# Loading weight blocks half a block before they are split, in a hybrid attention and retention layer

## The chip, the cores and the metric

The kernel runs on one core of a Trainium2 chip. The metric is the device time of one execution in microseconds (us), the median of several timed runs. The engines are TensorE (PE in the profile, with PEld for its weight loads), VectorE (DVE), ScalarE (ACT), GpSimd (POOL) and SyncE (SP), which here does nothing but issue transfers.

## The reference, cut to what matters

One decoder layer on a sequence of 1024 tokens with 1024 features, all float32:

```python
u = rmsnorm(x, norm_pre_w)
proj = u @ w_in                              # 1024 x 4096, eight parts of 512 columns
dq, dk, dv, dg, rq, rk, rv, rg = split(proj)
y_a = diff_attention(rotary(dq), rotary(dk), dv)   # 4 heads, two softmaxes each: p1 - lam * p2
y_a = rmsnorm(y_a, diff_subln_w) * (1 - lambda_init) * silu(dg)
y_b = retention(rotary(rq), rotary(rk), rv)        # 4 heads, chunks of 128 tokens, a state per chunk
y_b = rmsnorm(y_b) * silu(rg)
out = x + rmsnorm(concat(y_a, y_b) @ w_out, norm_post_w)
```

## The kernel before

Every float32 operand of a large product is split in two parts, hi (a cast to the type fp32r) and lo (the rest), and the product is three matmuls: hi by hi, lo by hi, hi by lo. The input tokens are split once (uh, ul, in two halves of 512 tokens).

The weights come in 16 blocks of 256 columns, in the order ORDER; a block is either values and gates of a head (part 0, `rows_steps`, matmuls of 256 columns) or queries and keys (part 1, `cols_steps`, matmuls of 512 columns). A block is four chunks of 256 KB. `load_chunk` issues the transfer of a chunk into one of four `raw` buffers, has ACT cast it to `whi`, and has DVE or POOL in turn subtract to get `wlo`. `whi` and `wlo` have eight buffers each, that is two blocks: a cast for block b+1 writes buffers that the matmuls of block b-1 read. `main_steps` calls `load_block(b + 1)` at the start of block b and then runs `block_steps(b)`, four groups g of matmuls, each into one PSUM bank.

The order of the instructions on PE and on SP's queue is the order of emission, which a planner in the kernel decides. It keeps an estimated time `clock[0]`, an estimate of SP's queue `queue[0]` (0.6 us for each transfer), and for each of the eight PSUM banks the estimated time at which it is free (`bank`, `give`). `run` takes `main_steps` as filler and puts steps of four side streams in as soon as they are due: `score_stream` (q by k matmuls, masked max, exponentials, the combined p), `value_stream` (`diff_turn` transposes p on PE at L524, `diff_values` multiplies by the values), `ret_stream` (retention: `ret_scores`, `ret_states`, `ret_out` at L617) and `last_stream` (`prep_tile` transposes finished rows, L672, for the output product of `out_steps`). Due times are `st["due", i]`, `due` and `st["y", t]`. The order on ACT, DVE and POOL is made by the compiler's own simulated schedule. All queues are in order: an instruction that waits holds those behind it.

Blocks 0 and 1 are emitted before `run`, with the planner's clock at 0 throughout. After the rotation of a query and key block, 24 small transfers (`moves` in `diff_qk`) per half of the tokens put hi and lo parts in place for the scores; they are held back by 4.0 us of estimated time (`late(4.0, moves)`). The output weights are loaded by `fetch_wout` and split by `split_wout` (`load_wout` is both); those of the first half of the output columns, `nh` 0, take over the buffers of uh0 and ul0, which the second group of block 15 is the last to read.

Of the kernel before, what the change touches and what calls it, by code (L numbers as in the profile page):

```python
# [10 lines left out]
F32 = mybir.dt.float32  # L11
# [9 lines left out]
P = 128  # L21
# [64 lines left out]
def body(ctx, tc, x, xt_in, pos, wpk, wout, vecs, npre, npost, subln, cst, out):  # L86
# [12 lines left out]
    wraw = pool("wraw", 4)  # L99
# [74 lines left out]
        eng = nc.vector if lo_turn[0] % 4 in (1, 2) else nc.gpsimd  # L174
        eng.tensor_tensor(dst, full, hi.bitcast(F32), op=ALU.subtract)  # L175

    def load_chunk(b, c, pieces=1):

        raw = wraw.tile([P, 2, 256], F32, tag="raw", name="raw")
        hi = whi.tile([P, 2, 256], F32R, tag="whi", name="whi")  # L180
        lo = wlo.tile([P, 2, 256], F32R, tag="wlo", name="wlo")
        for k in range(pieces):
            ks = slice(2 // pieces * k, 2 // pieces * (k + 1))
            dma(raw[:, ks, :], wpk[b, :, 2 * c + ks.start:2 * c + ks.stop, :])
            nc.scalar.copy(hi[:, ks, :], raw[:, ks, :])  # L185
            split_lo(lo[:, ks, :], raw[:, ks, :], hi[:, ks, :])
        return hi, lo

    def load_block(b):
        return [load_chunk(b, c) for c in range(4)]  # L190

    def weight(parts, kt):
        return tuple(part[:, kt % 2, :] for part in parts[kt // 2])
# [262 lines left out]
    def diff_scores(st, i, u):  # L456
# [52 lines left out]
        e1 = sm_.tile([P, 1], F32, tag="e1", name="e1")  # L509
        nc.vector.scalar_tensor_tensor(e1, s1, EPS, s1, op0=ALU.mult, op1=ALU.mult)  # L510
        st["p", i] = (p1, e1)
        st["due", i] = softmax[0] + 1.0

    def head_ms(o_ps, ms, scale):
        sq = sqp.tile([P, P], F32, tag="sq", name="sq")
# [197 lines left out]


    heads = [{"h": hh} for hh in HEADS]
    blocks = {}
    done = set()
    def block_steps(b):
        n, part = ORDER[b]
        st = heads[n]  # L720
        w = blocks[b]
        for g in range(4):

            if part == 0 and n > 2 and g == 0:
                yield lambda: ("A", n - 3) in done or ("R", n - 3) in done
            if part == 1 and n > 1 and g == 1:
                yield lambda: ("S", n - 2) in done or ("R", n - 2) in done
            if part == 0:
                ps = yield from rows_steps(w, g)
                values_gates(st, g, ps)  # L730
                st["values", g] = clock[0] + 1.44 + 1.6
                yield 1.44
            else:
                ps = yield from cols_steps(w, g % 2, g // 2)
                (diff_qk if st["h"] < H else ret_qk)(st, g, ps)
                yield 1.36
            if b == NB - 1:
                if g == 0:
                    load_wout(1, range(0, 4))
                elif g == 1:  # L740
                    load_wout(0, range(8))
                    fetch_wout(1, range(4, 8))
        blocks.pop(b)

    def main_steps():
        for b in range(2, NB):
            n, part = ORDER[b]
            if b + 1 < NB:
                blocks[b + 1] = load_block(b + 1)
            yield from block_steps(b)  # L750
        split_wout(1, range(4, 8))
        for t in range(NT):
            yield lambda: fp.get(("ready", t), 1e9) <= clock[0]
            yield from out_steps(t)
            done.add(("out", t))
# [35 lines left out]
    def ret_stream():  # L791
        for n, st in enumerate(heads):
            if st["h"] < H:
                continue
            for t2 in range(4):
                yield lambda: max(st.get(("ready", t2 // 2), 1e9), st.get(("values", t2), 1e9)) <= clock[0] and \
                    banks(2) and (n < 7 or "y" in fp and (t2 < 2 or ("prep", 2 * t2 - 3) in done))
                if n == 7:
                    load_y(2 * t2)
                    load_y(2 * t2 + 1)  # L800
                ret_scores(st, t2)
                due = clock[0] + 0.66 + 2.0
                yield 0.66
                yield lambda: due <= clock[0]
                ret_states(st, t2)
                due = clock[0] + 0.44 + 3.0
                yield 0.44
                yield lambda: due <= clock[0] and banks(1)
                ret_out(st, t2)
                for t in (2 * t2, 2 * t2 + 1):  # L810
                    st["y", t] = clock[0] + 0.88 + 4.5
                yield 0.88
            done.add(("R", n))

# [16 lines left out]
    def run(main, sides):  # L831

        sides = [[s, None] for s in sides]
        queue[0] = 8.0
        wait = None

        def advance(s):
# [33 lines left out]
    with tc.tile_pool(name="xin", bufs=6) as xin, tc.tile_pool(name="xp", bufs=1) as xp, tc.tile_pool(name="tp", bufs=1) as tp:  # L871
# [19 lines left out]
        for c in range(4):  # L891
            if c == 0:
                load_u(xin, 0, 0, 1)
                w0.append(load_chunk(0, c, 2))
                load_u(xin, 0, 1, 1)
            else:
                w0.append(load_chunk(0, c))
                load_u(xin, 0, 2 * c, 2)
        first = proj_rows(w0, [0, 1], [bank("pj"), bank("pj")])
        for c in range(4):  # L900
            load_u(xin, 1, 2 * c, 2)
        second = proj_rows(w0, [2, 3], [bank("pj"), bank("pj")])
        blocks[1] = load_block(1)
        dma(cs, cst)
        for half in range(2):
            dma(posi[64 * half:64 * half + 64, :], pos[half].partition_broadcast(64))
# [16 lines left out]
        nc.gpsimd.affine_select(out=tri, in_=tri, compare_op=ALU.is_ge, fill=0.0, base=0,  # L923
                                pattern=[[1, P]], channel_multiplier=-1)

        blocks[2] = load_block(2)
        for k, _ in enumerate(block_steps(1)):
            if k == 7:
                ec, es = angles(tp, posi, cs)
            if k == 11:  # L930
                tables(tp, ones, ec, es)
                nc.vector.tensor_scalar(wo["s"], sub, 0.5 * (1.0 - LAM_INIT), None, op0=ALU.mult)
                lambdas(tp, lv)
# [63 lines left out]
```

## Time and profile before

| what | value |
|---|---|
| time, median of 3 runs | 602.39 us (599.98 to 604.27) |
| the profiled execution: its own time, its span | 599.01 us, 597.3 us |
| PE busy | 575.7 us, 96% of the span |
| DVE, ACT, POOL busy | 52%, 41%, 23% |
| HBM, mean over the span | 77 GB/s |
| granted PE clock, mean | 0.994 |
| chain that ended last: PE, SP's queue, transfers | 77%, 7%, 7% |

PE is the engine to look at; the others matter where they make it wait. A row of a timeline shows in brackets how long its engine was idle before that instruction and what ended the wait.

### The profile page before, as it was taken

How to read it: one execution, taken by the hardware profiler on the slowest of the kernel's cores; microseconds unless marked ns; L12 is line 12 of the kernel's file. 1: busy time of each engine (PE TensorE's matmuls, PEld its weight loads, DVE VectorE, ACT ScalarE, POOL GpSimd, SP SyncE). 2: the span in 40 equal slices, each digit the busy share in tenths (PEclk: the TensorE clock that was granted, in tenths of full speed). 3: DMA queues.
4: the chain of work that ended last, by engine and by line, in shares of the span. 5: the costliest groups of instructions: out<-in, count | busy, mean ns of one | idle time of the engine just before them, and what ended most of it. 6: DMA issues, size and time to landing. Idle time of an engine off the chain costs nothing.

```text
span 597.3 us, 10157 instructions
## 1 busy us (share of the span) xinstructions
PE 575.7 (96%) x3664; PEld 521.0 (87%) x3664; DVE 307.9 (52%) x780; ACT 243.4 (41%) x700; POOL 136.1 (23%) x182
## 2 busy tenths in 40 slices
PE   6998997999999999999999999999999989999995
PEld 5998876999889988999899888899988988888884
DVE  3882247675542678522427784437585345443232
ACT  5796124355411664424026643126643454222120
POOL 3170133331321322312213223223220101000000
PEclk9999999999999999999999999999999999999998
DMA  8941645700214532212145332146401476243222
GB/s 274 371 162 36 175 103 151 181 19 19 80 27 105 156 103 58 74 46 81 36 122 128 97 98 54 32 101 156 119 16 39 122 247 215 71 151 121 73 72 105
DMA packets 41490, 65.62 MB, mean 110 GB/s; under 512 B 7136, under 2 KB 14688, under 8 KB 41440
## 3 DMA queue, kind: packets, MB, share of 16 engines
q1 hardware_dynamic: 41296, 64.97, 37.9%
q8 instruction: 29, 0.48, 0.3%
q14 instruction: 21, 0.17, 0.1%
q10 hardware_dynamic: 144, 0.00, 0.0%
HBM read 38.21 MB, written 7.86 MB: 77 GB/s over the span
## 4 chain that ended last, share of the span: by engine, by line
PE 77%; SPq 7%; DMA 7%; DVE 3%; ACT 2%; issue 2%; POOL 1%; DVEq 0%; POOLq 0%; ACTq 0%
PE pj L346 7%; PE pj L348 7%; PE pj L347 7%; SPq L123 7%; PE pj L360 7%; PE pj L362 7%; PE pj L361 7%; PE op L694 5%; PE op L692 5%; PE op L693 5%; PE sc L468 5%; PE o L537 5%; DMA raw<-in_wpk 4%; PE pj L329 3%; PE tp L524 3%; DMA raw<-in_wout 2%
## 5 line engine op out<-in xcount | busy, mean ns | idle before, releaser
L346 PE MATMUL pj<-whi,uh 128*128 128x256 f32 x448 | 129.4, 289 | 0.0
L348 PE MATMUL pj<-whi,ul 128*128 128x256 f32 x448 | 126.7, 283 | 0.0
L347 PE MATMUL pj<-wlo,uh 128*128 128x256 f32 x448 | 126.6, 283 | 0.0
L360 PE MATMUL pj<-uh,whi 128*128 128x512 f32 x256 | 103.0, 402 | 1.7 <-DVE gt L380 1.7
L362 PE MATMUL pj<-uh,wlo 128*128 128x512 f32 x256 | 100.5, 392 | 0.0
L361 PE MATMUL pj<-ul,whi 128*128 128x512 f32 x256 | 100.3, 392 | 0.0
L165 POOL TENSOR_TENSOR tot<-tot,halves 128x1 f32<-128x1 f32 (+1 forms) x56 | 34.2, 611 | 263.2 <-DVE tot L164 263.2
L346 PEld LDWEIGHTS pj<-whi,uh 128*128 128x128 f32 x448 | 85.6, 191 | 0.5 <-issue 0.2
L347 PEld LDWEIGHTS pj<-wlo,uh 128*128 128x128 f32 x448 | 85.7, 191 | 0.4
L348 PEld LDWEIGHTS pj<-whi,ul 128*128 128x128 f32 x448 | 85.6, 191 | 0.0
L175 POOL TENSOR_TENSOR wlo<-raw,whi 128x512 fp32r<-128x512 f32 x32 | 43.3, 1362 | 74.4 <-ACT whi L185 70.7
L185 ACT CAST whi<-raw 128x512 fp32r<-128x512 f32 (+1 forms) x65 | 39.1, 616 | 51.4 <-DMA raw<-in_wpk 44.4
L360 PEld LDWEIGHTS pj<-uh,whi 128*128 128x128 f32 x256 | 48.6, 190 | 11.0 <-DVE gt L380 1.9
L362 PEld LDWEIGHTS pj<-uh,wlo 128*128 128x128 f32 x256 | 48.3, 189 | 10.4
L361 PEld LDWEIGHTS pj<-ul,whi 128*128 128x128 f32 x256 | 48.6, 190 | 9.2
L493 ACT ACTIVATE p<-sc,nm 128x384 f32<-128x384 f32 (+5 forms) x48 | 27.6, 579 | 57.2 <-DVE nm L472 55.5
L692 PE MATMUL op<-woh,yh 128*128 128x512 f32 x128 | 50.8, 396 | 0.0
L694 PE MATMUL op<-woh,yl 128*128 128x512 f32 x128 | 50.0, 390 | 0.0
L693 PE MATMUL op<-wol,yh 128*128 128x512 f32 x128 | 49.9, 389 | 0.0
L468 PE MATMUL sc<-ks,qs 128*128 128x384 f32 (+5 forms) x192 | 43.3, 353 | 0.8 <-DMA qs<-rlo 0.8
L424 POOL TENSOR_TENSOR o<-o,m 128x512 f32<-128x512 f32 x16 | 25.9, 1622 | 77.1 <-DVE o L421 77.0
L698 ACT ACTIVATE osq<-op 128x512 f32<-128x512 f32 x16 | 9.6, 598 | 70.7 <-PE op L694 70.7
(138 smaller groups left out, 977.3 us busy)
## 6 DMA issues: line engine op xcount, KB each, us to landing
raw<-in_wpk SPq DMA_DIRECT2D x63, 256.0 KB, 4.4
xr<-in_x SPq DMA_DIRECT2D x8, 512.0 KB, 7.1
qs<-rhi SPq DMA_DIRECT2D x64, 64.0 KB, 2.0
qs<-rlo SPq DMA_DIRECT2D x64, 64.0 KB, 2.0
raw<-in_wout SPq DMA_DIRECT2D x16, 256.0 KB, 3.6
xt<-in_x SPq DMA_DIRECT2D x8, 512.0 KB, 3.6
out<-ob SPq DMA_DIRECT2D x16, 256.0 KB, 2.4
xk<-in_xt SPq DMA_DIRECT2D x7, 512.0 KB, 7.8
```

Source lines behind the costliest of these rows:

```text
L123: nc.sync.dma_start(dst, src)
L175: eng.tensor_tensor(dst, full, hi.bitcast(F32), op=ALU.subtract)
L346: nc.tensor.matmul(dst, lhsT=a, rhs=wh, start=(kt == 0 and j == 0), stop=False)
L347: nc.tensor.matmul(dst, lhsT=a, rhs=wl, start=False, stop=False)
L348: nc.tensor.matmul(dst, lhsT=b, rhs=wh, start=False, stop=(kt == KT - 1 and j == 1))
L360: nc.tensor.matmul(ps, lhsT=wh, rhs=uh[half][:, kt, :], start=(kt == 0), stop=False)
L361: nc.tensor.matmul(ps, lhsT=wh, rhs=ul[half][:, kt, :], start=False, stop=False)
L362: nc.tensor.matmul(ps, lhsT=wl, rhs=uh[half][:, kt, :], start=False, stop=(kt == KT - 1))
L468: nc.tensor.matmul(sp[:, 0:kn], lhsT=st["q"][:, u, x, i * P:(i + 1) * P], rhs=st["k"][:, u, k0:k0 + kn], start=(x == 0), stop=(x == 1))
L692: nc.tensor.matmul(op, lhsT=yh[:, m, :], rhs=wh, start=(m == 0), stop=False)
L693: nc.tensor.matmul(op, lhsT=yh[:, m, :], rhs=wl, start=False, stop=False)
L694: nc.tensor.matmul(op, lhsT=yl[:, m, :], rhs=wh, start=False, stop=(m == 7))
```

## The change

The transfer and the split of a chunk become two functions, `fetch_chunk` and `split_chunk`. The split of block b+1 stays at the start of block b; the transfers of block b+2 are issued in block b ahead of its third group (g == 2). The raw buffers stay four. For the output weights: chunks 0 to 3 of the second column half (`nh` 1) are fetched in block 14 and split at the start of block 15, and chunks 0 to 3 of the first column half are fetched after the first group of block 15 and split after its second. In block 1 the planner's clock now advances with the steps, and `run` shifts the banks' free times and starts again at 0. Three estimates are longer: p is due 0.5 us later, the retention output of the last head 1.0 us later, finished rows 1.5 us later.

```diff
--- before.py
+++ after.py
@@ -174,20 +174,31 @@
         eng = nc.vector if lo_turn[0] % 4 in (1, 2) else nc.gpsimd
         eng.tensor_tensor(dst, full, hi.bitcast(F32), op=ALU.subtract)
 
-    def load_chunk(b, c, pieces=1):
-
-        raw = wraw.tile([P, 2, 256], F32, tag="raw", name="raw")
+    raws, blocks = {}, {}
+
+    def fetch_chunk(b, c, pieces=1):
+
+        raw = raws[b, c] = wraw.tile([P, 2, 256], F32, tag="raw", name="raw")
+        for k in range(pieces):
+            ks = slice(2 // pieces * k, 2 // pieces * (k + 1))
+            dma(raw[:, ks, :], wpk[b, :, 2 * c + ks.start:2 * c + ks.stop, :])
+
+    def split_chunk(b, c, pieces=1):
+        raw = raws.pop((b, c))
         hi = whi.tile([P, 2, 256], F32R, tag="whi", name="whi")
         lo = wlo.tile([P, 2, 256], F32R, tag="wlo", name="wlo")
         for k in range(pieces):
             ks = slice(2 // pieces * k, 2 // pieces * (k + 1))
-            dma(raw[:, ks, :], wpk[b, :, 2 * c + ks.start:2 * c + ks.stop, :])
             nc.scalar.copy(hi[:, ks, :], raw[:, ks, :])
             split_lo(lo[:, ks, :], raw[:, ks, :], hi[:, ks, :])
         return hi, lo
 
-    def load_block(b):
-        return [load_chunk(b, c) for c in range(4)]
+    def fetch_block(b):
+        for c in range(4):
+            fetch_chunk(b, c)
+
+    def split_block(b):
+        blocks[b] = [split_chunk(b, c) for c in range(4)]
 
     def weight(parts, kt):
         return tuple(part[:, kt % 2, :] for part in parts[kt // 2])
@@ -509,7 +520,7 @@
         e1 = sm_.tile([P, 1], F32, tag="e1", name="e1")
         nc.vector.scalar_tensor_tensor(e1, s1, EPS, s1, op0=ALU.mult, op1=ALU.mult)
         st["p", i] = (p1, e1)
-        st["due", i] = softmax[0] + 1.0
+        st["due", i] = softmax[0] + 1.5
 
     def head_ms(o_ps, ms, scale):
         sq = sqp.tile([P, P], F32, tag="sq", name="sq")
@@ -713,13 +724,17 @@
 
 
     heads = [{"h": hh} for hh in HEADS]
-    blocks = {}
     done = set()
     def block_steps(b):
         n, part = ORDER[b]
         st = heads[n]
         w = blocks[b]
         for g in range(4):
+
+            if g == 2 and b + 2 < NB:
+                fetch_block(b + 2)
+            elif g == 2 and b + 2 == NB:
+                fetch_wout(1, range(0, 4))
 
             if part == 0 and n > 2 and g == 0:
                 yield lambda: ("A", n - 3) in done or ("R", n - 3) in done
@@ -736,9 +751,10 @@
                 yield 1.36
             if b == NB - 1:
                 if g == 0:
-                    load_wout(1, range(0, 4))
+                    fetch_wout(0, range(0, 4))
                 elif g == 1:
-                    load_wout(0, range(8))
+                    split_wout(0, range(0, 4))
+                    load_wout(0, range(4, 8))
                     fetch_wout(1, range(4, 8))
         blocks.pop(b)
 
@@ -746,7 +762,9 @@
         for b in range(2, NB):
             n, part = ORDER[b]
             if b + 1 < NB:
-                blocks[b + 1] = load_block(b + 1)
+                split_block(b + 1)
+            else:
+                split_wout(1, range(0, 4))
             yield from block_steps(b)
         split_wout(1, range(4, 8))
         for t in range(NT):
@@ -803,12 +821,12 @@
                 yield 0.66
                 yield lambda: due <= clock[0]
                 ret_states(st, t2)
-                due = clock[0] + 0.44 + 3.0
+                due = clock[0] + 0.44 + (4.0 if n == 7 else 3.0)
                 yield 0.44
                 yield lambda: due <= clock[0] and banks(1)
                 ret_out(st, t2)
                 for t in (2 * t2, 2 * t2 + 1):
-                    st["y", t] = clock[0] + 0.88 + 4.5
+                    st["y", t] = clock[0] + 0.88 + 6.0
                 yield 0.88
             done.add(("R", n))
 
@@ -831,7 +849,9 @@
     def run(main, sides):
 
         sides = [[s, None] for s in sides]
-        queue[0] = 8.0
+        for k in range(8):
+            free[k] -= clock[0]
+        clock[0], queue[0] = 0.0, 8.0
         wait = None
 
         def advance(s):
@@ -891,16 +911,19 @@
         for c in range(4):
             if c == 0:
                 load_u(xin, 0, 0, 1)
-                w0.append(load_chunk(0, c, 2))
+                fetch_chunk(0, c, 2)
+                w0.append(split_chunk(0, c, 2))
                 load_u(xin, 0, 1, 1)
             else:
-                w0.append(load_chunk(0, c))
+                fetch_chunk(0, c)
+                w0.append(split_chunk(0, c))
                 load_u(xin, 0, 2 * c, 2)
         first = proj_rows(w0, [0, 1], [bank("pj"), bank("pj")])
         for c in range(4):
             load_u(xin, 1, 2 * c, 2)
         second = proj_rows(w0, [2, 3], [bank("pj"), bank("pj")])
-        blocks[1] = load_block(1)
+        fetch_block(1)
+        split_block(1)
         dma(cs, cst)
         for half in range(2):
             dma(posi[64 * half:64 * half + 64, :], pos[half].partition_broadcast(64))
@@ -923,8 +946,10 @@
         nc.gpsimd.affine_select(out=tri, in_=tri, compare_op=ALU.is_ge, fill=0.0, base=0,
                                 pattern=[[1, P]], channel_multiplier=-1)
 
-        blocks[2] = load_block(2)
-        for k, _ in enumerate(block_steps(1)):
+        fetch_block(2)
+        split_block(2)
+        for k, cost in enumerate(block_steps(1)):
+            clock[0] += cost
             if k == 7:
                 ec, es = angles(tp, posi, cs)
             if k == 11:
```

## Rows read from the trace of the kernel before

**Rows 1.** Stretches of 15 us: length, busy (PE, PEld, DVE, ACT, POOL), clock, DMA share, GB/s

```profile
0.00:15.00 15.00, 9.72 (x59) 9.02 (x59) 6.03 (x10) 9.01 (x15) 4.92 (x14) 1.00 0.82 274
...
90.00:105.00 15.00, 11.30 (x48) 9.10 (x47) 10.62 (x32) 6.81 (x19) 5.92 (x4) 0.89 0.56 147
...
585.00:600.00 15.00, 6.05 (x27) 4.69 (x25) 3.00 (x6) 1.38 (x4) 0.55 (x1) 0.79 0.19 69
sum 600.00, PE 575.68 PEld 520.97 DVE 307.87 ACT 243.39 POOL 136.06; mean PE 14.39 PEld 13.02 DVE 7.70 ACT 6.08 POOL 3.40
```

**Rows 2.** Timeline of PE, the matmuls that it waited for after 15 us

```profile
57.67 0.50 PE L360 MATMUL pj<-uh,whi 128*128 128x512 f32 x1 [1.69 <-DVE gt L380]
...
83.11 0.30 PE L468 MATMUL sc<-ks,qs 128*128 128x128 f32 x1 [0.61 <-DMA qs<-rlo]
...
100.87 0.33 PE L524 MATMUL tp<-ident,p 128*128 128x128 f32 x1 [3.70 <-DVE p L508]
...
164.31 1.38 PE L524 MATMUL tp<-ident,p 128*128 128x128 f32 x8 [1.11 <-DVE p L508]
...
412.25 0.30 PE L524 MATMUL tp<-ident,p 128*128 128x128 f32 x1 [0.40 <-DVE e L510]
...
486.79 1.20 PE L672 MATMUL yt<-ident,yt 128*128 128x128 f32 x9 [0.72 <-DVE yt L396]
...
489.36 0.49 PE L617 MATMUL o<-v,sT 128*128 128x128 f32 x2 [1.15 <-DVE sT L594]
```

**Rows 3.** One stretch of 1 us, PE alone: length, busy, clock, DMA share, GB/s

```profile
102.00:103.00 1.00, 1.00 (x4) 0.50 0.64 141
```

**Rows 4.** Timelines of DVE and POOL ahead of the longest wait

```profile
93.47 0.69 DVE L175 TENSOR_TENSOR wlo<-raw,whi 128x512 fp32r<-128x512 f32 x1 [2.11 <-ACT whi L185]
...
95.28 0.29 DVE L472 CUSTOM_DVE_ANT_0 sc<-sc,mask 128x128 f32<-128x128 f32 x1
...
97.31 1.71 POOL L424 TENSOR_TENSOR o<-o,m 128x512 f32<-128x512 f32 x1
...
97.82 1.74 DVE L175 TENSOR_TENSOR wlo<-raw,whi 128x512 fp32r<-128x512 f32 x1
...
100.48 0.73 DVE L508 SCALAR_TENSOR_TENSOR p<-sc,cn,p 128x128 f32<-128x128 f32 x2
```

**Rows 5.** Timeline of SP's queue: issues of transfers

```profile
69.03 2.02 SPq L123 DMA_DIRECT2D raw<-in_wpk  x4
74.00 0.57 SPq L123 DMA_DIRECT2D ks<-rhi  x1
...
89.18 2.02 SPq L123 DMA_DIRECT2D raw<-in_wpk  x4
91.29 0.51 SPq L123 DMA_DIRECT2D ks<-rhi  x1
```

**Rows 6.** Transfers of one kind: count, KB each, median us to landing

```profile
qs<-rlo SPq DMA_DIRECT2D x64, 64.0 KB, 2.0
```

**Rows 7.** Who waited for whom: us in total, times, longest

```profile
POOL wlo L175 <- ACT whi L185: 70.7, 18, 9.5
...
ACT whi L185 <- DMA raw<-in_wpk: 44.4, 21, 15.7
```

**Rows 8.** The chain that ended last, 152 to 165 us: start, us, what

```profile
152.21 5.28 DMA raw<-in_wpk
...
158.27 3.08 POOL wlo L175 x2
...
163.60 0.67 DVE p L508
```

**Rows 9.** Timelines of ACT and DVE in block 15

```profile
484.96 2.71 ACT L651 ACTIVATE woh<-raw,wos 128x512 fp32r<-128x512 f32 x4 [3.90 <-DMA raw<-in_wout]
...
486.39 0.60 DVE L396 SCALAR_TENSOR_TENSOR yt<-o,tot,gt 128x128 f32<-128x128 f32 x2
...
488.89 0.41 DVE L594 TENSOR_TENSOR sT<-rs,tri 128x256 f32<-128x256 f32 x1
```

## The prediction

> **What bounds the kernel now.** I read the stretches first. Over the span of 597.3 us PE is busy 575.68 us [rows 1], so all that a change of order can give back lies in 21.6 us. Of those, 5.28 us are in the first 15 us (15.00 less 9.72, the first loads and splits) and 6.25 us at the end (the last stretch ends with the span after 12.30 us, 6.05 of them busy: the last evacuation and store) [rows 1]. The change touches neither, which leaves 10.1 us. The timeline of PE names them: seven waits of 1.69, 0.61, 3.70, 1.11, 0.40, 0.72 and 1.15 us, together 9.38 us [rows 2]; the rest are crumbs. One of them costs more than its length: in the stretch from 90 to 105 us the mean granted clock is 0.89, and right after the wait of 3.70 us it is 0.50, the lower of the two levels [rows 1, 3]. 0.11 of 15 us is 1.65 us of full-speed work that was lost. So the ceiling is 10.1 + 1.65, some 11.7 us or 2% of the kernel. What a reader is to see: 96% busy doesn't say where a gain can be; the bracketed waits do.
>
> Then I asked who holds PE up. The releaser is mostly DVE with the combined p, never a weight itself: after the start no weight load or split stands as the releaser of a matmul in these rows. Weights cost in another way. ACT stood 44.4 us, 21 times, before a cast whose transfer had not landed, once for 15.7 us, and POOL 70.7 us before the subtractions that follow [rows 7]. The queues are in order, so exponentials, row statistics and rotations stand behind those casts. The chain that ended last shows one such case whole: a weight transfer of 5.28 us, two subtractions of POOL in 3.08 us, then a row statistic, a scaling, and only then the p for which PE waits at 164 us [rows 8, 2].
>
> **The change part by part.** *Banks.* At 57.67 us, the first matmul of block 2, PE waits 1.69 us for the gates of block 1's last group [rows 2]. With the clock at 0 all banks of blocks 0 and 1 carry nearly the same free time, and the lowest number wins, which is the bank just used. With the clock running, block 2 opens with a bank whose reader belongs to block 0 and is long done. I take 1.6 us; ends 0 and 1.69. It is plain filler time, nothing else feeds those matmuls.
>
> *Loads of blocks 3 and up, around 57 to 107 us.* Here SP's queue is the critical chain. Four loads issue at 69.03 in 2.02 us, then nothing until 74.00, since the first `moves` need a cast that stands on ACT behind the casts of the weights just requested; 24 moves then take 89.18 - 74.00 = 15.18 us, 0.63 us each; then four more loads, and the next 24 moves begin at 91.29 [rows 5]. After the change the loads of block 3 are issued in block 1, where SP has little to do before the tables. The place at 69.03 goes to block 4's loads, whose buffers the early splits of block 3 have emptied. ACT is then not blocked, and the moves can start at 69.03 + 2.02 = 71.05, 2.95 us earlier. The four loads between the two sets of moves are gone, so the second set starts at 71.05 + 15.18 = 86.2, 5.1 us earlier than 91.29. A move lands some 2.0 us after its issue [rows 6]; the first score, which now waits 0.61 us, needs the twelfth: 71.05 + 12 x 0.63 + 2.0 = 80.6, while PE, 1.69 us earlier, comes to it at about 83.11 - 0.61 - 1.69 = 80.8. I take 0.3 us gained, ends 0 and 0.61.
>
> The wait at 100.87: DVE's score work starts at 95.28, after a subtraction at 93.47 for which DVE stood 2.11 us; then a second one, 1.74 us long, stands ahead of the statistics, and p is made at 100.48 [rows 4]. Freed of the waiting, and with the rotation buffers released some 3 us earlier, DVE can start the maxima 3 to 5 us earlier and p follows near 96. PE comes to the transpose at 100.87 - 3.70 = 97.2, less 1.7 for the banks and 0.3, plus 0.5 for the later due time: 95.7. So nearly all 3.70 us go, and with them the clock's 1.65. I take 4.9 of 5.35; the low end is 1.5, if only part of the wait goes and the clock falls all the same.
>
> *The same elsewhere.* The wait of 1.11 us at 164.31 goes: the transfer of 5.28 us leaves the chain [rows 8], four times the wait's length. I take 1.1, ends 0 and 1.11. The wait of 0.40 us at 412.25 I give whole, ends 0 and 0.40 [rows 2].
>
> *Block 15.* PE's waits of 0.72 and 1.15 us [rows 2] have one cause: ACT stands 3.90 us before the first output weights at 484.96, DVE stands behind it with their lo parts, and the scaling of the rows at 486.39 and the masked scores at 488.89 come late [rows 9]. The row names a transfer as releaser, but the casts write buffers that the second group of block 15 still reads, so I read PE as the true releaser. The earlier fetch can't help there. What helps are the estimates: the retention output 1.0 us later and finished rows 1.5 us later put block 15's own matmuls in PE's way instead. I take 1.7 of 1.87, the low end is 0. There is filler: the two remaining groups of block 15.
>
> **What it adds.** No arithmetic is added; the number of transfers is the same. (1) A fetch now waits on SP for raw buffers, that is for the splits of the block before; behind it on SP's queue stand row stores and the moves of the first half. In the chain of rows 8 the transfer, the idle time and the subtractions end at 161.35, 9.1 us after the transfer began, and half a block of matmuls plus the side streams is over 10 us; with the transfer gone from it the margin grows. I cost it at 0, ends 0 and 2. The late start of the moves (4.0 us of estimate) covers the four issues, 2.02 us [rows 5]. (2) A cast now waits only for the matmuls of the block before, no longer for data, so four casts and four subtractions come in a bunch at each block's start. A subtraction on DVE takes 0.69 us alone and 1.74 beside POOL [rows 4].
>
> The Trainium skill ("GPSIMD Engine Reference", section 8, Key points) says that POOL shares its SBUF interfaces with VectorE, in contention with VectorE instructions of two SBUF inputs, which a subtraction is. That speaks against bunching, and these two rows agree with it; by the rule the term of the next sentence would stand at its upper end of 3 us, and the sum below at 6.5 us instead of 9.0.
>
> Two DVE subtractions a block cost 2 x 1.05 = 2.1 us more if both collide. DVE is busy 307.87 of 597.3 us [rows 1], so I let PE see 0.5 us in all, ends 0 and 3. (3) With PE some 8 us earlier, the scores of the second half of the tokens come up against SP's queue: its last move issues at 86.2 + 15.2 = 101.4. No row prices that; between 0 and the landing of one move, 2.0 [rows 6], I take 0.5.
>
> *Sum.* 1.6 + 0.3 + 4.9 + 1.1 + 0.4 + 1.7 = 10.0 gained, 1.0 given back: 9.0. The profiled execution took 599.0 us, 590.0 after. The median of the runs is 602.39, 0.56% above the profiled one; 590.0 x 1.0056 = 593.3, say 593. A change of 1% is 6.0 us, about what three runs between 599.98 and 604.27 can tell from none.
>
> **The rivals.** *Half of it.* SP's queue stays the bound up to 107 us: PE no longer waits at 100.87 for p, but the order on DVE is simulated anew and may still put a collided subtraction ahead. 2 us of that wait stay and the clock still falls (1.7 gained instead of 4.9), the second half's scores wait the full 2.0, the rest holds: 10.0 - 3.2 - 2.5 = 4.3 gained, 594.7, or 598 on the scale of the runs. For it: 76 of the 80 issues there remain. Against: the two gaps of SP in rows 5 are explained by loads that move.
>
> The Trainium skill ("Perfetto Trace Analysis", What "DMA-bound" means) counts an issuing sequencer that is solid with DMA slices as a bound of its own, whatever the data. By it this rival gains weight, since rows 5 show 24 issues with hardly a gap.
>
> *It does nothing.* The waits only move: with PE's order drawn up anew, each removed wait is replaced by another of its size, as filler runs out elsewhere. 602, within 3.
>
> *Slower.* The casts wait for PE. No transfer sets their time now, so the simulated schedule puts all four at the instant at which it thinks the block before ends. Where it thinks so too early, ACT stands with the exponentials behind it. If that delays p by 5 us or more, like the transfer in rows 8, PE waits 1.1 us [rows 2] and the clock may fall for 1.65 [rows 1]: 2.75 at each of the 13 block starts from block 3 on is 36 us, at half of them 18. Less the 3.3 that banks and block 15 still give, half of them means 613.7, or 617. It decides against the change from 4 block starts on (11 us, more than the 10.0). Against it: the eight buffers made the same wait possible before.
>
> **How the numbers follow.** Forecast 0.52, half 0.26, nothing 0.13, slower 0.09. With the seven waits gone, the crumbs too, and nothing given back, 10.1 + 1.65 = 11.7 us, the time is 587.3, or 590.6; runs spread by 0.36% either way, so the low end is 588.5. The high end takes in the half case and part of the third: 602.5. Faster by over 1% (below 596.4): most of the first and a third of the second, 0.57. Slower by over 1%: 0.09. Within: 0.34.
>
> **What would show it.** Right: PE's first matmul of block 2 without a wait; ACT's wait for weight transfers from 44.4 us down to a few after the start; on SP one set of loads, then 48 moves without loads between; no stretch of clock 0.50 near 100 us; no waits of PE in block 15 above 0.3 us. Wrong: new rows with PE waiting for q or k transfers near 105 us, ACT casts released by PE for a microsecond and more, or DVE subtractions of 1.7 us ahead of each p.

## The result and the profile after

The changed kernel takes 591.46 us (median of 6 runs, 590.35 to 593.45) beside 599.9 us (6 runs, 596.15 to 604.27) for the kernel before: a ratio of 0.986, 95% interval 0.9812 to 0.9907. The forecast was 593.0 with 588.5 to 602.5. Its profiled execution took 590.74 us with a span of 588.9 us, where the one before had 597.3: 8.4 us less, forecast 9.0. These are single executions; another one of the changed kernel took 593.81 us (below).

The timeline of PE in the changed kernel, the matmuls that it waited for after 15 us; it answers to [rows 2]. The bracket is the idle time ahead of the matmul and what ended it.

```profile
81.31 0.30 PE L479 MATMUL sc<-ks,qs 128*128 128x128 f32 x1 [0.40 <-DMA ks<-rlo]
82.44 0.33 PE L479 MATMUL sc<-ks,qs 128*128 128x128 f32 x1 [0.83 <-DMA qs<-rlo]
113.75 0.41 PE L585 MATMUL tp<-ident,kT 128*128 128x128 f32 x2 [1.50 <-DMA kT<-o]
114.44 0.68 PE L592 MATMUL rs<-qT,kT 128*128 128x128 f32 x4 [0.27 <-DMA qT<-o]
246.81 2.02 PE L548 MATMUL o<-v,at 128*128 128x128 f32 x16 [0.81 <-DVE y L407]
331.49 1.16 PE L548 MATMUL o<-v,at 128*128 128x128 f32 x8 [0.83 <-DVE y L407]
```

Six of the seven waits of [rows 2] are gone; the seventh, at the first score, has grown from 0.61 to 0.40 + 0.83 = 1.23 us. Four are new. Their sum is 4.64 us, where it was 9.38.

The stretches of 15 us of the changed kernel (columns as in [rows 1]), those that changed and the sum:

```profile
75.00:90.00 15.00, 13.77 (x62) 11.03 (x61) 6.28 (x11) 3.47 (x7) 4.48 (x4) 1.00 0.53 130
90.00:105.00 15.00, 15.00 (x75) 12.58 (x74) 11.30 (x38) 5.09 (x18) 3.91 (x4) 1.00 0.44 101
105.00:120.00 15.00, 13.23 (x109) 12.82 (x108) 10.46 (x32) 9.13 (x30) 5.71 (x7) 1.00 0.62 154
...
480.00:495.00 15.00, 15.00 (x103) 13.80 (x103) 9.50 (x22) 7.21 (x20) 0.90 (x2) 1.00 0.55 193
...
sum 600.00, PE 572.69 PEld 519.64 DVE 311.51 ACT 244.93 POOL 135.22; mean PE 14.32 PEld 12.99 DVE 7.79 ACT 6.12 POOL 3.38
```

Between 90 and 105 us PE is busy throughout at a clock of 1.00, where 11.30 us at 0.89 stood [rows 1]. The start has not moved (PE busy 9.70 us of the first 15, where it was 9.72). PE's idle time is 588.9 - 572.69 = 16.2 us; it was 597.3 - 575.68 = 21.6 [rows 1]. So of the 8.4 us, 5.4 are idle time and 3.0 are shorter busy time, some 1.65 of that being the clock (0.11 of 15 us).

Who waited for whom in the changed kernel (total, times, longest, in us); it answers to [rows 7]:

```profile
POOL wlo L175 <- ACT whi L192: 63.0, 16, 10.6
...
ACT whi L192 <- PE pj L372: 18.4, 18, 3.7
...
ACT rhi L446 <- DMA sinR<-B: 14.6, 1, 14.6
...
ACT whi L192 <- DMA raw<-in_wpk: 9.7, 11, 1.6
```

ACT's wait for weights fell from 44.4 us with a longest of 15.7 [rows 7] to 9.7 with a longest of 1.6. But the longest one has mostly changed its name: at the same place ACT now stands 14.6 us before a rotation's cast (rhi), for a transfer of a table of sines. In the kernel with the banks alone, its loads as before, the total is 31.4 us with a longest of 4.6, and 15.7 stand before the rotation's cast. The casts now wait 18.4 us for matmuls of PE, where it was 4.1 (6 times, 0.8 at the longest).

SP's queue in the changed kernel, which answers to [rows 5]; all issues between these rows are the 48 moves of q and k, hardly a gap among them:

```profile
70.87 1.97 SPq L123 DMA_DIRECT2D raw<-in_wpk  x4
73.39 0.57 SPq L123 DMA_DIRECT2D ks<-rhi  x1
...
88.65 0.54 SPq L123 DMA_DIRECT2D ks<-rhi  x1
...
104.35 2.03 SPq L123 DMA_DIRECT2D raw<-in_wpk  x4
106.47 0.50 SPq L123 DMA_DIRECT2D kT<-o  x1
```

There is one set of loads and then all moves, as forecast, but the first move comes at 73.39 and not at 71.05. The next loads come at 104.35, after the last move, and the transfers of k for the retention (kT) stand behind those.

### The profile page after: what moved, and what is told of

Same layout as the page of the kernel before. It is cut to its first block, busy times and chain, and to the rows that moved or that the text cites. A ratio compares the mean times of both kernels' runs of the same rounds, so it can differ in the third digit from the quotient of the medians.

```text
span 588.9 us, 10174 instructions
## 1 busy us (share of the span) xinstructions
PE 572.7 (97%) x3664; PEld 519.6 (88%) x3664; DVE 311.5 (53%) x780; ACT 244.9 (42%) x700; POOL 135.2 (23%) x182
## 4 chain that ended last, share of the span: by engine, by line
PE 81%; DMA 5%; ACT 4%; SPq 4%; DVE 3%; issue 2%; POOL 0%; DVEq 0%; POOLq 0%; ACTq 0%
PE pj L371 8%; PE pj L373 8%; PE pj L372 8%; PE pj L357 7%; PE pj L359 7%; PE pj L358 7%; PE o L548 5%; PE sc L479 5%; PE op L705 5%; PE op L703 5%; PE op L704 5%; SPq L123 4%; PE tp L535 2%; DMA raw<-in_wpk 2%; DMA xk<-in_xt 1%
## 5 line engine op out<-in xcount | busy, mean ns | idle before, releaser
L373 PEld LDWEIGHTS pj<-uh,wlo 128*128 128x128 f32 x256 | 48.0, 188 | 10.4
L175 POOL TENSOR_TENSOR wlo<-raw,whi 128x512 fp32r<-128x512 f32 x32 | 41.7, 1313 | 66.5 <-ACT whi L192 63.0
L192 ACT CAST whi<-raw 128x512 fp32r<-128x512 f32 (+1 forms) x65 | 39.2, 617 | 31.8 <-PE pj L372 18.4
L548 PEld LDWEIGHTS o<-v,at 128*128 128x128 f32 x288 | 36.6, 191 | 3.7 <-DVE y L407 1.2
```

The source lines that it names most:

```text
L373: nc.tensor.matmul(ps, lhsT=wl, rhs=uh[half][:, kt, :], start=False, stop=(kt == KT - 1))
L548: nc.tensor.matmul(o_ps[:, 0:P], lhsT=at[:, j * P:(j + 1) * P], rhs=v[:, j0 + j, :], start=(j0 + j == 0), stop=(j0 + j == i))
```

## The experiments

Two theories stood at the start. **A, the prediction's:** early data frees ACT and SP, which removes the waits at 100 and 164 us; the banks remove the one at 57, the estimates those of block 15; so the parts add up. **Z, the rival:** what counts is that PE's order is drawn up anew, so the estimates and banks do it and the early loads hardly matter. Each kernel is compared with the kernel before on its chip (602.0 to 602.5 us).

**Banks alone**, on the kernel before:

```
-        queue[0] = 8.0
+        for k in range(8):
+            free[k] -= clock[0]
+        clock[0], queue[0] = 0.0, 8.0
...
-        for k, _ in enumerate(block_steps(1)):
+        for k, cost in enumerate(block_steps(1)):
+            clock[0] += cost
```

> The kernel before with one part of the change alone: the planner's clock advances in block 1 and is shifted to 0 at the start of the planned part. Theory A (the parts add up, each by the wait that it removes): the wait of 1.69 us at the first matmul of block 2 goes, all other waits stay, the time falls by 1.5 to 1.9 us. Theory Z (what counts is that the order is drawn up with more slack, the rest is small): within 1 us of the kernel before.

Measured: 600.18 us, ratio 0.9958 (0.9926 to 0.9990). PE's timeline, its first score and the p that it waits for near 100 us:

```profile
82.49 0.30 PE L468 MATMUL sc<-ks,qs 128*128 128x128 f32 x1 [2.06 <-DMA ks<-rlo]
83.64 0.44 PE L468 MATMUL sc<-ks,qs 128*128 128x128 f32 x1 [0.85 <-DMA qs<-rlo]
100.91 0.33 PE L524 MATMUL tp<-ident,p 128*128 128x128 f32 x1 [1.70 <-DVE p L508]
```

The wait of 1.69 us in block 2 is gone, but PE only comes earlier to the first score and waits 2.91 us there instead of 0.61, and the clock falls to 0.89 in the stretch from 75 us. A bank's wait ahead of a transfer's wait is no gain of its own here. The other waits did not stay, as theory A had it: the one near 100 us is 1.70, one of 0.72 us at 184.60 is new, the one at 412 us is 1.55, and block 15 has one of 0.42 left.

**Estimates alone**, on the kernel before:

```
-        st["due", i] = softmax[0] + 1.0
+        st["due", i] = softmax[0] + 1.5
...
-                due = clock[0] + 0.44 + 3.0
+                due = clock[0] + 0.44 + (4.0 if n == 7 else 3.0)
...
-                    st["y", t] = clock[0] + 0.88 + 4.5
+                    st["y", t] = clock[0] + 0.88 + 6.0
```

> The kernel before with the three longer estimates alone (p due 0.5 us later, retention output of the last head 1.0, finished rows 1.5). Theory A: the two waits of block 15 go (1.87 us), of the 3.70 us near 100 us at most 0.5 goes and the clock still falls there, so the time falls by 1.7 to 2.5 us. Theory Z: the longest wait and the one of 1.11 us at 164 go too, the time falls by 6 us or more.

Measured: 597.72 us, 0.9893 (0.9846 to 0.9939). PE's timeline near 100 us:

```profile
100.77 0.47 PE L524 MATMUL tp<-ident,p 128*128 128x128 f32 x1 [3.26 <-DVE p L508]
```

The waits at 164 us, at 412 us and in block 15 are gone without a single load being earlier. The one at 100 us stays, with a clock of 0.83 in the stretch from 90 us. Waits of 0.79, 0.87, 0.68, 0.35 and 1.48 us come up between 329 and 435 us. The gain, 4.5 us between the medians, lies between the two forecasts.

**Early loads alone** (the changed kernel with the two edits above undone):

> The kernel before with the early loads alone, of weight blocks and of output weights; banks and estimates as before. Theory A: the wait of 3.70 us with the lower clock (5.35 us), those of 1.11 and 0.40 us go; a new one of 1 to 2 us comes where retention's q and k transfers stand behind the loads; the waits at block 2's start and in block 15 stay; the time falls by 4 to 6 us. Theory Z: by less than 2 us.

Measured: 593.78 us, 0.9844 (0.9796 to 0.9892). PE's timeline at block 2, and the stretch behind it:

```profile
58.61 0.50 PE L371 MATMUL pj<-uh,whi 128*128 128x512 f32 x1 [2.11 <-DVE gt L391]
...
60.00:75.00 15.00, 15.00 (x61) 12.21 (x61) 4.04 (x6) 1.10 (x2) 1.67 (x1) 0.90 0.66 166
```

The bank's wait is back and the clock falls behind it, to 0.90 in this stretch. The waits at 100 and 164 us are gone. So are those of block 15: PE is busy 15.00 of 15 us from 480 us on, with the old estimates. New are 0.68 us before kT at 115.30 and four waits of 0.64 to 0.83 us between 181 and 426 us. The gain, 8.4 us between the medians, is more than theory A's 4 to 6.

**Banks and estimates, loads as before** (the first two edits together):

> Banks and estimates together, loads as before the change: the changed kernel without its early loads. Theory A: faster than before by 3.4 to 4.2 us, so slower than the changed kernel by 4 to 5 us, with a wait of 3 us or more near 100 us. Theory Z: within 2 us of the changed kernel.

Measured: 595.24 us, 0.9854 (0.9814 to 0.9894). PE's timeline near 100 us:

```profile
99.51 0.33 PE L524 MATMUL tp<-ident,p 128*128 128x128 f32 x1 [2.76 <-DVE p L508]
```

This wait stays, with a clock of 0.89 in the stretch from 90 us. In time, theory Z's forecast came true (within 2 us of the changed kernel) and A's (4 to 5 us slower than it) did not; in the waits, A's nearly did (2.76 us near 100 us for "3 us or more"). Neither theory stands whole. The three parts alone give 0.42, 1.07 and 1.56%, together 3.05, while all of them in one kernel give 1.4 (the result) or 1.7 (below): the parts don't add up. One reason is in the traces: the waits at 164 us and in block 15 can each be removed by two of them. Early loads alone (0.9844) and the other two parts without them (0.9854) each reach about what all three reach. Nor do the medians show what the early loads add to the other two (0.9854 without them, 0.986 and 0.983 with them): they take the wait at 100 us and bring those for kT and y. But in the traces here the wait at 100 us is gone only where the data are early; the banks alone shorten it to 1.70 us, and banks with estimates leave 2.76.

**The same program again**, beside its variants:

> The changed kernel once more, beside the next three. All theories: 0.986 of the kernel before, within 0.5%.

Measured: 592.55 us, 0.9830 (0.9795 to 0.9864). The profiled execution took 593.81, with this in PE's timeline and in its stretch:

```profile
115.21 0.41 PE L585 MATMUL tp<-ident,kT 128*128 128x128 f32 x2 [3.10 <-DVE wlo L175]
...
105.00:120.00 15.00, 11.78 (x82) 11.36 (x82) 7.94 (x23) 6.94 (x22) 5.70 (x7) 0.89 0.62 156
```

The wait of 1.50 us at the same matmul of the first trace is 3.10 us here, and the clock falls with it. The row names a subtraction of DVE as releaser, but the transfers of kT fit better. These are the four of this stretch, from issue to landing:

```profile
DMA to landing us min/median/max: 4.0/6.6/7.1
```

The first matmul needs the first two. The second of them is issued at 108.22 us and lands 6.9 us later, at 115.1; in the first trace it is issued at 107.71 and lands 5.9 us later, at 113.6. In all five traces with this wait (these two, the early loads alone, and two more below, whose rows name DVE as well) PE starts 0.13 to 0.14 us after that landing.

In both executions the early loads are not early here. Requested half a block ahead in the order, they come up on SP behind the 48 moves, at 104.86 us (104.35 in the first trace), and ACT stands up to 2.36 us before a weight cast (1.52), DVE up to 3.62 us before a subtraction (2.51).

**Loads of the retention's blocks a quarter block later**, behind the transfers that their heads wait for:

```
-            if g == 2 and b + 2 < NB:
+            at = 3 if part == 1 and st["h"] >= H else 2
+            if g == at and b + 2 < NB:
```

> The changed kernel, but in the query and key blocks of retention the loads are issued ahead of the fourth group instead of the third, so behind the first four small transfers to kT and qT. Theory L (PE's wait of 1.50 and 0.27 us near 114 us is kT's and qT's transfers standing behind 1 MB of weights in the DMA engines): a kT transfer near 105 us lands 2 to 3 us after its issue instead of 6, the wait goes, the time falls by 1 to 2 us. Rival (the rotation or the order on SP is late there in any case): the wait stays above 1 us and the time within 0.5 us of the changed kernel.

Measured: 591.64 us, 0.9821 (0.9785 to 0.9857). PE's timeline where the kT wait stood:

```profile
115.88 0.62 PE L479 MATMUL sc<-ks,qs 128*128 128x384 f32 x2 [0.45 <-ACT kr L587]
...
118.93 0.39 PE L357 MATMUL pj<-whi,uh 128*128 128x256 f32 x1 [0.55 <-DVE y L407]
```

The wait for kT is gone, two smaller ones of 1.00 us together stand nearby, and the clock stays at 1.00. The two transfers that PE needs first now land 2.3 us after their issue. Position in the queue caused that wait. The median is 0.9 us under that of the changed kernel on the same chip, inside the uncertainty.

**All loads a quarter block ahead** instead of half a block (`g == 3` for `g == 2`):

> The changed kernel with the loads ahead of the fourth group of every block: a quarter of a block ahead of the split instead of half. Theory A (what counts is that the data is there when the split starts, and at block 2 the loads then stand behind 24 small transfers): ACT waits for weight transfers more than 20 us in total, and a wait of PE of over 1 us near 100 us comes back; slower than the changed kernel by 1 to 4 us. Rival D (any distance of some microseconds does): within 1 us of the changed kernel.

Measured: 595.1 us, 0.9869 (0.9838 to 0.9901). PE's timeline, the waits view, and the loads of blocks 3 and 4 on SP's queue:

```profile
99.58 0.48 PE L535 MATMUL tp<-ident,p 128*128 128x128 f32 x1 [2.75 <-DVE p L519]
...
ACT whi L192 <- DMA raw<-in_wpk: 24.1, 19, 4.9
...
69.34 3.54 SPq L123 DMA_DIRECT2D raw<-in_wpk  x4
...
88.84 1.97 SPq L123 DMA_DIRECT2D raw<-in_wpk  x4
```

With half the lead the wait at 100 us is back, at 2.75 us, and the clock with it (0.89 from 90 us on), and ACT waits 24.1 us for weights instead of 9.7. On SP's queue nothing is left of the lead at this place: the loads of block 3 stand behind the tables and those of block 4 between the two sets of moves, at 69.34 and 88.84 us, where the kernel before has them at 69.03 and 89.18 [rows 5]. So the run shows that this wait hangs on when the loads are issued, as theory A has it; how much lead would do, it does not show.

**Output weights as before** (the first four not fetched in block 14, no early split):

```
-            elif g == 2 and b + 2 == NB:
-                fetch_wout(1, range(0, 4))
...
-                    fetch_wout(0, range(0, 4))
+                    load_wout(1, range(0, 4))
...
-                    split_wout(0, range(0, 4))
-                    load_wout(0, range(4, 8))
+                    load_wout(0, range(8))
...
-            else:
-                split_wout(1, range(0, 4))
```

> The changed kernel with the output weights loaded and split where the kernel before has it; weight blocks, banks and estimates as changed. Theory P (the prediction's: the estimates remove block 15's waits, the early output loads cannot help): no wait of PE above 0.3 us between 480 and 495 us, the time within 0.5 us of the changed kernel. Rival O (the early output loads remove them): waits of 1 to 2 us together in block 15, slower by as much.

Measured: 594.59 us, 0.9858 (0.9821 to 0.9895). PE's timeline in block 15, and ACT ahead of the first wait:

```profile
472.60 0.71 PE L604 MATMUL rs<-v,kr 128*128 128x128 f32 x4 [0.91 <-ACT kr L587]
481.98 0.71 PE L604 MATMUL rs<-v,kr 128*128 128x128 f32 x4 [0.16 <-ACT kr L587]
...
470.00 0.72 ACT L662 ACTIVATE woh<-raw,wos 128x512 fp32r<-128x512 f32 x1 [3.55 <-DMA raw<-in_wout]
...
472.19 0.35 ACT L587 COPY kr<-tp 128x256 f32<-128x256 f32 x1
```

Between 480 and 495 us, where 0.72 + 1.15 stood [rows 2], only 0.16 us come back, as theory P has it. But block 15 begins near 459 us in this trace, and the 0.91 us at 472.60 lie in it: the copy (kr) for which PE waits stands on ACT behind the casts of the output weights, which waited 3.55 us for their transfer. Together that is 1.07 us, the 1 to 2 us of rival O. The median is 2.0 us above the changed kernel's on the same chip, inside the uncertainty; the longer wait for kT (1.71 us at 114.14, with a clock of 0.89) is part of the trace's difference.

**The subtractions of the weights all on DVE**, on top of the late loads of the retention:

```
-            split_lo(lo[:, ks, :], raw[:, ks, :], hi[:, ks, :])
+            nc.vector.tensor_tensor(lo[:, ks, :], raw[:, ks, :], hi[:, ks, :].bitcast(F32), op=ALU.subtract)
```

> The kernel with retention's loads late, and every subtraction of the weight splits on DVE instead of every other one on POOL. Theory C (two POOL subtractions of 1.3 us in a row hold up the powers that follow on POOL, and DVE's operations take 1.7 us beside them): DVE's weight subtractions have a median of 0.69 and none above 1.3 us, the waits for y near 247 and 332 us go, DVE's busy time rises by 32 x 0.69 = 22 us less what the collisions cost, and the time is 1 to 2 us lower. Rival (DVE has no room at a block's start): p comes late, new waits of PE for DVE of 1 us and more, slower by 1 to 5 us.

Measured: 587.35 us (587.02 to 587.86), 0.9753 (0.9738 to 0.9767), the fastest kernel here. PE's timeline, the matmuls that it waited for after 15 us, and the weights' subtractions by tile (min/median/max in ns):

```profile
82.04 0.33 PE L479 MATMUL sc<-ks,qs 128*128 128x128 f32 x1 [0.81 <-DMA qs<-rlo]
...
114.89 0.61 PE L479 MATMUL sc<-ks,qs 128*128 128x384 f32 x2 [0.28 <-ACT kr L587]
...
L193 DVE TENSOR_TENSOR wlo<-raw,whi x65: 419/686/775, 5.2 to 420.6; 128x512 fp32r<-128x512 f32 x63, 128x256 fp32r<-128x256 f32 x2
```

Both waits for y are gone. No subtraction takes over 0.775 us, though DVE has 326.5 us to do instead of 312.0 in the kernel with the late loads of the retention. The gain over that kernel (0.9821) is some 4 us, more than the 1 to 2 expected.

**The same with the retention's loads where the change has them:**

> The changed kernel with all weight subtractions on DVE, retention's loads not late. Theory C with theory L: the waits for y near 247 and 332 us go, those behind the loads near 114 us stay at 1 to 3 us, so between the changed kernel and the one with both edits: 0.976 to 0.981 of before. Rival: the same as with both edits, 0.975.

Measured: 588.7 us, 0.9766 (0.9725 to 0.9806). The y waits are gone here too, and a wait of 0.85 us at the first matmul of kT, at 113.41, is back. So most of the gain comes from the subtractions; what the later loads add is inside the uncertainty.

**The same edit on the kernel before:**

> The kernel before the change with all weight subtractions on DVE, loads as before. Theory A (near 100 us the late data holds DVE; POOL's part is only behind the waits near 164 us and smaller ones): the wait of over 2 us with the lower clock near 100 us stays, 1 to 3 us faster than before. Rival C2 (POOL's subtractions were the cause all along, and early loads matter little): the wait near 100 us goes, 6 us faster or more.

Measured: 603.38 us, 1.0018 (0.9993 to 1.0044), a miss of the 1 to 3 us expected. PE near 100 us, and DVE ahead of it:

```profile
101.62 0.47 PE L524 MATMUL tp<-ident,p 128*128 128x128 f32 x1 [4.16 <-DVE p L508]
...
93.81 0.69 DVE L186 TENSOR_TENSOR wlo<-raw,whi 128x512 fp32r<-128x512 f32 x1 [6.00 <-ACT whi L185]
```

With late data DVE stands 6.00 us before a subtraction, with all row statistics behind it, instead of 2.11 [rows 4]. Subtractions on DVE pay only once the data are early.

**Banks of the outputs called free 2 us later**, on top of the late loads of the retention (`0.222 * nb + 7.5` for `+ 5.5`):

> The kernel with retention's loads late, and the bank of the attention output counted as free 2.0 us of estimate later (7.5 instead of 5.5). Theory Y (PE's two waits of about 0.8 us near 247 and 332 us are for a bank that the scaling of rows on DVE has not yet read, since subtractions and rotations bunched at a block's start stand ahead of it): both waits go, 1.5 us faster than with retention's loads late alone, 0.980 of the kernel before. Rival (the step is only held back by as much): within 0.5 us of it, 0.982.

Measured: 590.12 us, 0.9807 (0.9782 to 0.9833). PE's timeline where the largest wait now stands:

```profile
364.12 2.02 PE L548 MATMUL o<-v,at 128*128 128x128 f32 x16 [1.38 <-DVE tot L164]
```

The y waits are gone, but this one, 0.86 us at 115.60 and two small ones take their place: 2.8 us in all, where 0.45 + 0.55 + 0.81 + 1.13 = 2.9 stood. The time does not tell the two theories apart (0.980 and 0.982 were expected). Planning around the wait moves it; the subtractions on one engine remove it.

## Why the prediction came out right

The sign, the size and most of the mechanism held: 9.0 us forecast, 8.4 measured. That the sum came so close is partly luck: what was given back is four times the forecast, and 2.0 us of the gain belong to no term. By its own terms, in the profiled executions:

**Gained, forecast 10.0.** *Banks*, 1.6: 1.69 gone at block 2 (alone they only moved it, as shown above). *The wait at 100 us with the clock*, 4.9: all 5.35 gone. The forecast chain is in the changed kernel's timeline of DVE, which answers to [rows 4]:

```profile
92.25 0.29 DVE L483 CUSTOM_DVE_ANT_0 sc<-sc,mask 128x128 f32<-128x128 f32 x1
...
95.80 0.74 DVE L519 SCALAR_TENSOR_TENSOR p<-sc,cn,p 128x128 f32<-128x128 f32 x2
```

The maxima start at 92.25 us instead of 95.28, p at 95.80 instead of 100.48 ("p follows near 96"), both within the 3 to 5 us forecast. *164 and 412 us*, 1.5: both waits gone, 1.51. *Block 15*, 1.7: all 1.87 gone. The five give 10.4.

**The step on the first score failed.** Forecast: 0.3 us gained, as the moves would start at 71.05. Measured: 0.62 lost. The claim that ACT would then not be blocked held for the weights only; a transfer that the step did not look at became the last to come. ACT's timeline of the changed kernel:

```profile
72.75 1.14 ACT L446 CAST rhi<-o 128x512 fp32r<-128x512 f32 x2 [14.65 <-DMA sinR<-B]
```

The first cast of the rotated rows waits for the last table of sines, until 72.75 us, and the moves follow at 73.39. The early loads are not the reason: in the kernel with the banks alone, its loads as before, the same cast waits 15.69 us for the same table, until 72.79. The table lands at 72.5 us in both; in the kernel before it landed at 70.8, and the cast of a weight held ACT until 72.83. Why it lands later, and why the cast of these rows, which are rotated with other tables, waits for it, stays open. The second set of moves began at 88.65, not 86.2.

**Given back, forecast 1.0.** Term (1), the fetch on SP, was costed at 0 with ends 0 and 2, and measured 1.77 us (1.50 + 0.27), 3.10 and the clock in another execution. This is the step that was mis-sized most. I looked for row stores and moves behind the loads on SP and missed the retention's transfers, which come right after them. In the changed kernel the kT transfers of this stretch, from issue to landing:

```profile
L123 SPq DMA_DIRECT2D kT<-o x4: 461/522/554, 106.5 to 110.6; - x4
...
DMA to landing us min/median/max: 5.0/5.8/6.0
```

They take 5.8 us in the median, over the whole kernel 2.3: the loads ahead of them are 1 MB. The variant with the retention's loads later shows the cause: 2.3 us to landing, and no wait. The Trainium skill ("Perfetto Trace Analysis", What "DMA-bound" means) counts an issuing sequencer that is solid with issues as a bound of its own. SP is solid from 73.39 to 107 us, but this was not what PE waited for. The scores of the second half had no wait, and the second kT transfer was issued at 107.71 us, earlier than in the kernel before (109.64, landed 2.3 us later); it landed at 113.6 and not at 111.9 because the loads stood ahead of it.

Term (2), bunched subtractions and collisions, was put at 0.5 with ends 0 and 3, and measured 0.81 + 0.83 = 1.64 us. DVE and POOL of the changed kernel ahead of the wait at 246.81:

```profile
242.53 1.30 POOL L175 TENSOR_TENSOR wlo<-raw,whi 128x512 fp32r<-128x512 f32 x1
243.78 0.21 POOL L557 TENSOR_TENSOR tot<-tot,rs 128x1 f32<-128x1 f32 x1
244.20 1.66 POOL L435 TENSOR_TENSOR o<-o,m 128x512 f32<-128x512 f32 x1
...
244.64 1.77 DVE L434 TENSOR_TENSOR o<-o,m 128x512 f32<-128x512 f32 x1
246.33 0.85 DVE L407 SCALAR_TENSOR_TENSOR y<-o,tot,gt 128x128 f32<-128x128 f32 x3
```

The row scalings (y), whose banks PE needs, stand behind a rotation of DVE that takes 1.77 us beside POOL's. They also need a factor (tot) that POOL makes in several short steps, and two of the bunched subtractions on POOL, at 240.09 and 242.53, stand ahead of and between these. The kernel with the subtractions all on DVE and the retention's loads late tells the two apart:

```profile
239.53 0.18 POOL L557 TENSOR_TENSOR tot<-tot,rs 128x1 f32<-128x1 f32 x1
...
240.84 0.86 DVE L407 SCALAR_TENSOR_TENSOR y<-o,tot,gt 128x128 f32<-128x128 f32 x3
...
243.61 1.76 DVE L434 TENSOR_TENSOR o<-o,m 128x512 f32<-128x512 f32 x1
```

The factor is ready 4.3 us earlier (the rotation starts 1.0 us earlier), three scalings run ahead of the rotation, and PE does not wait, though the rotation still takes 1.76 us beside POOL's. So the collision by itself does not make the first wait; POOL's subtractions ahead of its own short steps do, with the order on DVE that follows from them. Ahead of the second, at 331.49, two subtractions hold POOL for 2.76 us from 325.96 and no rotation runs at all. The prediction priced slow subtractions on DVE; the nearest ones of DVE ahead of the two waits took 0.68 us each. The term's size lay inside its ends, its mechanism was another one. The Trainium skill ("GPSIMD Engine Reference", section 8, Key points) says that POOL contends with VectorE instructions of two SBUF inputs at their shared interfaces. The two rotations of 1.76 and 1.77 us beside POOL's agree, but they are not what PE waited for. Term (3), second-half scores, was put at 0.5 and measured 0.

In sum 10.4 gained and 0.62 + 1.77 + 1.64 = 4.0 given back make 6.4 us. The other 2.0 of the 8.4 are 0.7 us of crumbs and 1.3 us of PE's busy time beyond the clock, which I can't place (ends of matmuls are modelled in the records).

**Two attributions failed** that the time did not show. "The earlier fetch can't help there" of block 15: the kernel with early loads and the old estimates has no waits there, and with the output loads alone put back, 0.91 us stand there behind the casts of the output weights. How much of the first is the fetch is not settled, since in that kernel the whole order ahead of block 15 is another one. And the sum took each wait as owned by one part; the waits at 164 us and in block 15 have two remedies each.

**The slower rival's mechanism exists**, but costs no wait for p: the casts wait 18.4 us for PE, up to 3.7 at a time, and PE has no wait for p in the changed kernel. **The rival "it does nothing"** was partly right: waits do come up elsewhere, 4.0 us of them.

## What to carry to other kernels

Ask of each load that is issued earlier not only what it frees but which small, urgent transfers now stand behind it, on the issuing queue and in the DMA engines; and whether it is really earlier there, or only in the order of the program. Parts of a change that cure the same wait don't add up, so time them alone and together before crediting one. A releaser that a row names can be a bystander: compare it with the landing times of the transfers that the instruction needs. Once the data were early here, how the work is shared between DVE and POOL was the next limit, and an edit worth nothing before (1.0018) was then worth over half a per cent (0.9753 beside 0.9821).

## What the runs showed of the hardware

A rotation's difference of 128x512 on DVE (line 434) takes 0.68 us at the least in the changed kernel, and 1.77 us where a rotation of POOL runs beside it (244.64). The longest of the sixteen is 1.78 to 1.79 us with the weights' subtractions on POOL and without them. Their median is 0.892 us in the changed kernel, 0.684 with the subtractions off POOL, but also 0.682 with them on POOL in the kernel before, so it does not tell what the subtractions cost.

A transfer of 128 KB (kT) issued right behind four loads of 256 KB landed 5.0 to 6.0 us after its issue in the changed kernel and 4.0 to 7.1 in its second execution; issued ahead of them (the retention's loads late), the first two took 2.3 us.

The granted clock stayed at 1.00 over the stretch with PE's waits of 1.50 us (the changed kernel, 113.75) and 1.70 us (banks alone, 100.91), and was 0.83 to 0.90 in the stretch with or behind waits of 2.11, 2.75, 2.76, 3.10 and 3.26 us. The length alone doesn't tell it: with the output weights as before a wait of 1.71 us at 114.14 came with 0.89. And the waits of 0.72 and 1.15 us in block 15 of the kernel before left the stretch from 480 us at 1.00, where 0.73 and 1.15 us at the same two matmuls, with the subtractions on DVE, came with 0.91.

A program's waits differ between executions: the same matmul of the same program waited 1.50 us in one and 3.10 us in the other, and the whole execution took 590.74 and 593.81 us.
